# A two-layer decoder trunk: route weights made earlier, alpha·x taken off the matmuls, a fixed order for the layer norm into mixer 1

## The chip, the cores and the metric

The kernel runs on one core of one Trainium2 chip. The metric is the device time of one execution in microseconds (us). Engines are named as in the profile: PE is TensorE's matmuls, PEld its weight loads, DVE is VectorE, ACT is ScalarE, POOL is GpSimd, SP is SyncE, whose queue issues the transfers.

## The reference

256 tokens of 1024 features pass through two layers, all in fp32. Each layer is a mixer and a mixture of experts, and each of these is followed by a layer norm over its input, scaled by alpha, plus its output:

```python
for layer in range(2):
    mix = ab_mixer(x, ...) if layer % 2 == 0 else nsa_mixer(x, ...)
    x = layer_norm(DN_ALPHA * x + mix, ln1_g[layer], ln1_b[layer])
    ffn = hier_moe(x, ...)          # 32 experts in 4 groups, each token routed to 2 of one group
    x = layer_norm(DN_ALPHA * x + ffn, ln2_g[layer], ln2_b[layer])
```

`ab_mixer` is a gated MLP beside a latent attention, `nsa_mixer` an attention with three branches (compressed blocks, selected blocks, window) whose compressed keys and values come from two small networks with weights of their own. `hier_moe` softmaxes the group logits, takes the best group and its top two experts, and gives each expert's output a weight ("route weight" below).

## The kernel before

**Weights and the ring.** All weights come from HBM in slots of 1 MB (128 partitions x 2048 fp32). SBUF holds a ring of 23 places of that size. `Ring` issues the slots on SP's queue at L124, one after the other in the order of a list: for a mixer the string `ORDER[l]`, for the experts slots 0 to 11 of each of eight quads of four experts (`QUADS`). A slot's issue waits until the place it goes to has been freed, and everything behind it on the queue waits too. An entry `P` of `ORDER` is no transfer but a place taken as working space (for the high and low halves of split weights); names such as `CK0`, `QA`, `X` or `xTh` in it are slots or working places too.

**Products.** An fp32 product is made of three products of halves (`mm3`): each operand is split into a rounded high part and the rest. `Splits` makes the halves of a weight, the high part on ACT (L311), the low part on DVE or POOL (L312). All matmuls have the line of the helper `mm`, L182, so that the tile names tell them apart.

**A layer.** Mixer 0 and mixer 1 run under a scheduler (a plan with costs decides the order of their pieces). At their end `project` multiplies the mixer's output by the output weights `WO0..3` into four PSUM accumulators `acc[t][h]` (t: tokens 0 to 127 or 128 to 255; h: columns 0 to 511 or 512 to 1023); its first step opens each accumulator with alpha·x, matmuls of x with `aident`, alpha times the identity. `close_mixer` finishes it: `raw(t)` copies the accumulators to x and takes the statistics of the layer norm, then come the router's logits, `route`, which selects the experts and returns a function that makes the route weights later (L1254 to L1264, 8 small DVE steps and 3 on ACT for each half of the tokens), `rank`, and the first `pick`. `places` makes a one-hot matrix of the tokens of a quad; `pick` multiplies it with x to gather these tokens (`w`, 32 rows an expert); the affine part of the norm (L493) and the second half of the first pick are done in between.

**The experts.** For each quad in turn: `gate_up` (k = 0..7, one slot each, slots 0 to 7, `psC<-ring,w`; after each k a function `between(k)` puts other work in), `activate`, `pick` for the next quad (`psT<-p,x`), `turn_hidden`, `back` (which weights the one-hot matrix by the route weights at L1393, turns it with two matmuls at L1397, and makes the weights of the slots' tokens with `psO<-oneh,p`), and then the down product (slots 8 to 11, `psT<-ring,p`), whose results go back to the tokens in `acc2` (psA, psS). Quad 0 differs: after its gate_up, `rest()` makes the route weights of both halves and `back` for quad 0, and after `turn_hidden` four matmuls with `aident` per token half and column half (`psA<-x,aident`, `psS<-x,aident`; an fp32 matmul of 512 columns is two instructions in the trace) add alpha·x to `acc2`, which had been opened with zeros in `close_mixer` (`zerob`).

**Between the layers.** `open_mixer1` makes the layer norm (`ln2`: L562 and L571, two DVE steps for a half of a token half, with one of four such quarters on ACT and POOL at L568 to L570), transposes each quarter (`transpose_x`: PE L329, ACT L332, DVE L333), and makes the first product of mixer 1, `project(t, low, xk)`, with the narrow weights `NAT`, whose halves are made on ACT (L843, four of 128x608) and POOL (L878). `warm(n)` gives PE n matmuls whose result nobody reads; `W3` says how many stand here, behind the first and the second quarter. In the same stretch the scheduler already splits weights `KVC` and `KSW` for mixer 1 (L311, L312).

Of the kernel before, what the change touches and what calls it, by code (L numbers as in the profile page):

```python
# [24 lines left out]
KC = D // 128  # L25
# [17 lines left out]
W3 = (7, 6)  # L43
# [99 lines left out]
def trunk(ctx, tc, a, out):  # L143
# [109 lines left out]
    aident = consts.tile([128, 128], F32, name="aident")  # L253
    idb = consts.tile([128, 128], BF16, name="idb")
    zerob = consts.tile([128, 128], BF16, name="zerob")
# [11 lines left out]
    def more_constants():  # L267
        V.memset(mhalf, -0.5)
        V.memset(mone, -1.0)
        V.memset(oneh, 1.0)  # L270
        V.memset(oneb, 1.0)
        V.memset(zerob, 0.0)
        V.tensor_scalar(aident, ident, ALPHA, None, op0=ALU.mult)
        V.tensor_copy(maskb, tri[:, 128:256])
        V.tensor_copy(trib, tri[:, 0:128])
# [172 lines left out]
    def project(l):  # L448
# [27 lines left out]
    def close_mixer(l, rb, acc, step, products):  # L476
# [50 lines left out]
        for h in range(2):  # L527
            mm(acc2[0][h], zerob, idb[:, None, :].to_broadcast([128, 4, 128]), True, False)
        warm(2)
# [5 lines left out]
        for h in range(2):  # L535
            mm(acc2[1][h], zerob, idb[:, None, :].to_broadcast([128, 4, 128]), True, False)
        warm(W1[0])
# [297 lines left out]
    def open_mixer1(acc, g, b, mr):  # L835

        wn = []
        for i in range(4):
# [4 lines left out]
            S.activation(hi, src, AF.Copy)  # L843
# [16 lines left out]
        late = []  # L860

        def after(t, h):
            low = transpose_x(xh, xl, t, h)
            if late:
                late.pop()()
            late.append(low)
            if (t, h) == (0, 0):
                warm(W3[0])
            if (t, h) == (0, 1):
                warm(W3[1])  # L870
                project(0, 0, xh)
            if (t, h) == (1, 0):
                project(0, 0, xl)

        ln2(acc, g, b, mr, after)
        late.pop()()
# [3 lines left out]
        project(1, 0, xh)  # L880
        project(1, 0, xl)
# [508 lines left out]
    def back(q, rt, dd, tr, often=True):  # L1390

        d, dw = dd[:, 0:256], (p2() if dd.shape[1] == 256 else dd[:, 256:512])[:, 0:256]
        V.tensor_tensor(dw.rearrange("p (t e s) -> p t e s", t=2, e=4), d.rearrange("p (t e s) -> p t e s", t=2, e=4),  # L1393
                        rt[1][:, :, 4 * q:4 * q + 4, None].to_broadcast([128, 2, 4, 32]), op=ALU.mult)
        p = ps(tr)
# [13 lines left out]
    def gather(q, rt, base, tr):  # L1409
# [5 lines left out]
        return xg, *back(q, rt, dd, tr, often)  # L1415
# [62 lines left out]
    def moe_layer(l, rt, acc, begun):  # L1478
# [3 lines left out]
        gs, late = [(begun[0], None, None)], begun[1:]  # L1482
# [7 lines left out]
        def quad(i):  # L1490
# [4 lines left out]

            def between(k):
                nonlocal rb
                if i == 0 and k >= KC // 2:
                    late[0].pop(0)()
                    if k == KC - 1:  # L1500
                        late[0].pop(0)()
                if k in (2, 4):
                    flush(2)
                if k == 4:
                    dds.append(places(nq, rt, 0.0))
                if k == 5 and i == 3 and l == 0:
# [3 lines left out]
            if i == 0:  # L1510
                gs = [late[1]()]
            hs = activate(hp, [g[2] for g in gs])
            ngs, hts = [], None
            for c in range(nn):
                xg = halves_of(w4())
                pick(dds[c], xg)()
                if c + 1 < nn:
                    dds.append(places(nq, rt, -32.0 * (c + 1)))
                if c == 0:
                    hts = turn_hidden(hs)  # L1520
                    if i == 0:
                        for t in range(2):
                            for h in range(2):
# [169 lines left out]
```

## Time and profile before

| | |
|---|---|
| median of 3 runs | 700.41 us (700.06 to 701.95) |
| the profiled execution | 700.38 us, its span 698.7 us |
| mean granted TensorE clock | 0.956 |
| busy, of the span | PE 619.1 us, DVE 284.3, ACT 204.5, POOL 49.6 |
| moved by DMA | 235.62 MB, mean 337 GB/s |

The profile is that of one execution; its own time is 1.7 us over its span. The times of all rows below are counted from the start of the span. At the 420 GB/s of the stretches in which DMA is full, the 235.62 MB would take 561 us; PE is busy for 619 us. Neither fills the span: there are stretches in which the one waits for the other.

### The profile page before, as it was taken

How to read it: one execution, taken by the hardware profiler on the slowest of the kernel's cores; microseconds unless marked ns; L12 is line 12 of the kernel's file. 1: busy time of each engine (PE TensorE's matmuls, PEld its weight loads, DVE VectorE, ACT ScalarE, POOL GpSimd, SP SyncE). 2: the span in 40 equal slices, each digit the busy share in tenths (PEclk: the TensorE clock that was granted, in tenths of full speed). 3: DMA queues.
4: the chain of work that ended last, by engine and by line, in shares of the span. 5: the costliest groups of instructions: out<-in, count | busy, mean ns of one | idle time of the engine just before them, and what ended most of it. 6: DMA issues, size and time to landing. Idle time of an engine off the chain costs nothing. (4 is left out here: it accounts for less than half of the span.)

```text
span 698.7 us, 11137 instructions
## 1 busy us (share of the span) xinstructions
PE 619.1 (89%) x4459; PEld 386.7 (55%) x4459; DVE 284.3 (41%) x709; ACT 204.5 (29%) x514; POOL 49.6 (7%) x56
## 2 busy tenths in 40 slices
PE   7799999799999685887999999999799899897883
PEld 5678676464555141423988776685554554644331
DVE  4757736522222120206848897444422212312116
ACT  5554534121111010103546676431111111202011
POOL 4611000000000000002420000000000000000002
PEclk9999999989999988997999999999899999999797
DMA  8946879949999999999498450399689999999961
GB/s 344 418 184 247 334 264 380 398 189 425 419 420 418 423 420 416 421 420 416 161 422 342 127 235 1 129 394 401 280 353 420 420 422 421 420 419 422 414 266 60
DMA packets 34068, 235.62 MB, mean 337 GB/s; under 512 B 3920, under 2 KB 4688, under 8 KB 6224
## 3 DMA queue, kind: packets, MB, share of 16 engines
q1 hardware_dynamic: 34000, 234.75, 82.7%
q8 instruction: 38, 0.62, 0.4%
q14 instruction: 30, 0.25, 0.1%
HBM read 233.69 MB, written 1.05 MB: 336 GB/s over the span
## 5 line engine op out<-in xcount | busy, mean ns | idle before, releaser
L182 PE MATMUL psC<-ring,w 128*32 128x512 f32 (+1 forms) x1040 | 132.5, 618 | 24.5 <-PEq L1299 13.1
L182 PEld LDWEIGHTS psC<-ring,w 128*32 128x32 f32 (+1 forms) x1040 | 31.2, 114 | 90.0 <-issue 48.5
L182 PE MATMUL psA<-ring,ring 128*128 128x256 f32 (+1 forms) x480 | 80.1, 315 | 0.0
L182 PE MATMUL psT<-ring,p 128*32 128x512 f32 (+1 forms) x608 | 68.8, 587 | 3.1 <-DMA ring<-in_moe 2.2
L182 PEld LDWEIGHTS psA<-ring,ring 128*128 128x128 f32 x480 | 67.5, 193 | 6.5 <-issue 1.8
L182 PEld LDWEIGHTS psT<-p,x 128*128 128x128 f32 x512 | 64.5, 208 | 10.9 <-issue 10.1
L182 PE MATMUL psT<-p,x 128*128 128x128 f32 x512 | 67.3, 295 | 0.0
L1437 DVE SCALAR_TENSOR_TENSOR p<-p,psC 128x256 f32<-128x256 f32 x16 | 6.7, 421 | 133.5 <-ACT p L1436 133.3
L317 DVE TENSOR_TENSOR p<-psT,p 128x256 fp32r<-128x256 f32 x72 | 30.5, 424 | 62.8 <-ACT p L316 62.8
L1436 ACT ACTIVATE p<-psC 128x256 f32<-128x256 f32 x16 | 6.1, 383 | 170.2 <-PE psC L182 170.2
L316 ACT ACTIVATE p<-psT 128x256 fp32r<-128x256 f32 x72 | 27.5, 383 | 63.2 <-PE psT L182 42.2
L290 POOL TENSOR_TENSOR sm<-sm,mhalf 128x1 f32<-128x1 f32 (+1 forms) x12 | 7.7, 647 | 511.4 <-DVE sm L287 280.6
L182 PEld LDWEIGHTS psA<-p,k 128*128 128x128 f32 x144 | 25.2, 192 | 30.1 <-issue 17.6
L182 PE MATMUL psA<-p,k 128*128 128x256 f32 x144 | 39.4, 313 | 1.6 <-DVE sm L1560 1.6
L312 DVE TENSOR_TENSOR ring<-ring,ring 128x1024 fp32r<-128x1024 f32 (+1 forms) x28 | 36.0, 1301 | 8.0 <-ACT ring L311 7.7
L182 PEld LDWEIGHTS psT<-ring,p 128*32 128x32 f32 x608 | 17.3, 111 | 37.6 <-issue 25.3
L182 PE MATMUL psS<-ring,ring 128*128 128x416 f32 (+3 forms) x128 | 32.0, 384 | 2.0 <-ACT ring L311 1.5
L182 PE MATMUL psO<-ring,ring 128*64 128x256 f32 (+3 forms) x248 | 32.2, 349 | 1.1 <-DVE ring L333 0.7
L311 ACT ACTIVATE ring<-ring 128x1024 fp32r<-128x1024 f32 (+1 forms) x32 | 31.8, 1031 | 3.6 <-issue 1.3
L182 PE MATMUL psS<-p,k 128*128 128x256 f32 x144 | 29.9, 288 | 0.0
L1377 DVE COPY w<-psT 128x512 f32<-128x512 f32 x16 | 11.1, 691 | 44.2 <-PE psT L182 44.2
L1111 ACT ACTIVATE ring<-psS,sm 128x128 f32<-128x128 f32 (+1 forms) x64 | 26.2, 420 | 7.8 <-DVE sm L1102 7.7
(282 smaller groups left out, 844.4 us busy)
## 6 DMA issues: line engine op xcount, KB each, us to landing
ring<-in_moe SPq DMA_DIRECT2D x192, 1024.0 KB, 19.5
ring<-in_m SPq DMA_DIRECT2D x23, 1024.0 KB, 10.0
ring<-in_vec SPq DMA_DIRECT2D x2, 1024.0 KB, 18.1
ring<-in_m SPq DMA_DIRECT2D x2, 832.0 KB, 6.0
x<-in_x SPq DMA_DIRECT2D x2, 512.0 KB, 5.2
out<-x SPq DMA_DIRECT2D x4, 256.0 KB, 2.0
ring<-in_m SPq DMA_DIRECT2D x1, 768.0 KB, 15.0
ring<-in_m SPq DMA_DIRECT2D x1, 736.0 KB, 18.9
```

The costliest lines, as they stand in the source:

```text
L182: T.matmul(o, lhsT, rhs, start=start, stop=stop, skip_group_check=True)
L290: G.tensor_tensor(r, t, mhalf[:, :n], op=ALU.pow)
L311: S.activation(hi, src, AF.Copy)
L312: (sub or V).tensor_tensor(lo, src, hi.bitcast(F32), op=ALU.subtract)
L316: S.activation(hi, src, AF.Copy)
L317: V.tensor_tensor(lo, src, hi.bitcast(F32), op=ALU.subtract)
L1111: S.activation(p[:, i * w:(i + 1) * w], sx[c, u][:, i * w:(i + 1) * w], AF.Exp, bias=nb[:, i0 + i:i0 + i + 1], accum_out=su[:, i0 + i:i0 + ...
L1377: (S.activation(dst, p[0], AF.Copy) if f == 0 else V.tensor_copy(dst, p[0]))
L1436: S.activation(e, p[:, 0:256], AF.Tanh, scale=0.5)
L1437: V.scalar_tensor_tensor(e, e, 1.0, p[:, 0:256], op0=ALU.add, op1=ALU.mult)
```

## The change

It has four parts.

1. **alpha·x without matmuls.** The `aident` matmuls go. In `project` the first product opens the accumulator, and `raw(t)` computes x = alpha·x + acc on DVE, with the statistics then taken from x in SBUF. For the experts, ACT writes alpha·x into `acc2` (`residual`), for columns 0 to 511 during quad 0's gate_up at k = 7, for the others after `back`. The matmuls with `zerob` that opened `acc2` become as many more `warm` matmuls.
2. **Route weights early.** `rest` is split: `shares`, called at k = 1 of quad 0's gate_up, makes the route weights and the weighted one-hot matrix of quad 0; `back` comes after gate_up as before, without the weighting. For the later quads the weighted matrix is made at k = 4 (`onehots`).
3. **Into mixer 1.** `ln2` isn't called: all four quarters of the norm are two DVE steps each (`halves`), in an order written out with the transposes, products and ACT's high halves; the low halves of `NAT` move from POOL to DVE; `W3` falls from 7 and 6 to 4 and 3. A `no_sync_barrier` (an order for the scheduler, no wait on the chip) keeps mixer 1's own pieces behind it.
4. **The list of layer 1.** `CK0` and `CK1` come before `QA Y Q1`, `CV1` and `CV0` a little earlier too. Smaller: `router_prep` of layer 1 moves from quad 3 to quad 5 of layer 0, and the scratch for dynamic DMA is 1024 in place of 512.

```diff
-W3 = (7, 6)
+W3 = (4, 3)
...
-         "NAT1 P P NAT0 P KSW xTl xTh P P KVC P Q0 P P X Z P QA Y Q1 P P P CK0 CK1 CV1 CV0 Q2 P P QB Q3 M P M  "
+         "NAT1 P P NAT0 P KSW xTl xTh P P KVC P Q0 P P X Z CK0 CK1 QA Y Q1 CV1 P P CV0 P P Q2 P P QB Q3 M P M  "
...
         def products(t, i):
             k = ks[i]
-            if i == 0:
-                for h in range(2):
-                    mm(acc[t][h], aident, x[:, t, HALF[h]], True, False)
...
-                mm3(acc[t][h], y, w, False, i == KC - 1)
+                mm3(acc[t][h], y, w, i == 0, i == KC - 1)
...
         def raw(t):
 
             for h in range(2):
-                S.activation(x[:, t, HALF[h]], acc[t][h], AF.Copy)
-            return x[:, t], *stats(acc[t])
+                V.scalar_tensor_tensor(x[:, t, HALF[h]], x[:, t, HALF[h]], ALPHA, acc[t][h], op0=ALU.mult, op1=ALU.add)
+            return x[:, t], *stats([x[:, t, HALF[h]] for h in range(2)])
...
-        def rest():
+        def shares():
             weights0()
             weights1()
-            return (xg, *back(0, rt, dd, "O"))
-
-        return rt, acc2, (xg, [second] + affines, rest)
+            return weighted(0, rt, dd, p2()[:, 0:256])
+
+        return rt, acc2, (xg, [second] + affines, shares, lambda dw: (xg, *back(dd, dw, "O")))
...
+        def halves(t, h):
+
+            xs, (mean, r) = x[:, t, HALF[h]], mr[t]
+            V.scalar_tensor_tensor(xs, acc[t][h], mean, g[:, HALF[h]], op0=ALU.subtract, op1=ALU.mult)
+            V.scalar_tensor_tensor(xs, xs, r, b[:, HALF[h]], op0=ALU.mult, op1=ALU.add)
+            late[t, h] = transpose_x(xh, xl, t, h)
...
+        high(0)
+        halves(0, 0)
+        warm(W3[0])
+        high(1)
+        halves(0, 1)
+        warm(W3[1])
+        high(2)
+        high(3)
+        project(0, 0, xh)
+        halves(1, 0)
+        late[0, 0]()
+        halves(1, 1)
+        late[0, 1]()
+        project(1, 0, xh)
+        project(0, 0, xl)
+        late[1, 0]()
+        late[1, 1]()
+        project(1, 0, xl)
         for hi, lo, src, _ in wn:
-            G.tensor_tensor(lo, src, hi.bitcast(F32), op=ALU.subtract)
+            V.tensor_tensor(lo, src, hi.bitcast(F32), op=ALU.subtract)
...
+            def residual(h):
+                for t in range(2):
+                    S.activation(acc[t][h], x[:, t, HALF[h]], AF.Copy, scale=ALPHA)
+
+            def onehots(c):
+                dd = places(nq, rt, -32.0 * c)
+                dds.append((dd[:, 0:256], weighted(nq, rt, dd[:, 0:256], dd[:, 256:512])))
+
             def between(k):
                 nonlocal rb
+                if i == 0 and k == 1:
+                    late[1] = late[1]()
                 if i == 0 and k >= KC // 2:
                     late[0].pop(0)()
                     if k == KC - 1:
                         late[0].pop(0)()
+                        residual(0)
...
             if i == 0:
-                gs = [late[1]()]
+                gs = [late[2](late[1])]
...
                     hts = turn_hidden(hs)
-                    if i == 0:
-                        for t in range(2):
-                            for h in range(2):
-                                mm(acc[t][h], aident, x[:, t, HALF[h]], False, False)
-                ngs.append((xg, *back(nq, rt, dds[c], "O")))
+                ngs.append((xg, *back(*dds[c], "O")))
+            if i == 0:
+                residual(1)
...
             m = open_mixer1(acc, *gb, mr)
+        tc.no_sync_barrier()
         mixer1(*m)
```

The first place where the order changes is PE's row at the end of gate_up of quad 0, layer 0 (psC is gate_up's accumulator, psO what `back` makes, psT first the pick and then the down product). Before:

```order
L182 MATMUL psC_1136<-ring_699,w_152_1121 32x512 x4
L1397 MATMUL psO_1251<-ident,k_149_1112 128x128 x2
L182 MATMUL psO_1251<-oneh,p_163_1249 128x1 x2
L182 MATMUL psT_1265<-p_158_1175,x 128x128 x8
L182 MATMUL psT_1275<-p_158_1175,x 128x128 x8
L1449 MATMUL psC_1285<-ident,p_167_1260 128x128 x2
L182 MATMUL psA_1033<-x,aident 128x512
L182 MATMUL psA_1034<-x,aident 128x512
L182 MATMUL psS_1035<-x,aident 128x512
L182 MATMUL psS_1036<-x,aident 128x512
L1397 MATMUL psO_1294<-ident,p_158_1175 128x128 x2
L182 MATMUL psO_1294<-oneh,p_158_1175 128x1 x2
```

and after the change:

```order
L182 MATMUL psC_1128<-ring_695,w_152_1113 32x512 x4
L1400 MATMUL psO_1246<-ident,k_149_1104 128x128 x2
L182 MATMUL psO_1246<-oneh,p_156_1155 128x1 x2
L182 MATMUL psT_1260<-p_159_1189,x 128x128 x8
L182 MATMUL psT_1270<-p_159_1189,x 128x128 x8
L1452 MATMUL psC_1280<-ident,p_167_1255 128x128 x2
L1400 MATMUL psO_1284<-ident,p_159_1189 128x128 x2
L182 MATMUL psO_1284<-oneh,p_159_1189 128x1 x2
L182 MATMUL psT_1295<-ring_697,p_167_1255 32x512 x4
```

The four matmuls with `aident` are gone between `turn_hidden` (psC from ident) and the next quad's `back`; the matmul with `oneh` now reads a matrix (`p_156`) that was made during gate_up. The same holds for layer 1.

The second place is DVE's row over the same gate_up (`rt` and `w_121` are the route weights, `w_152` the first pick, the lines on x the affine part of the norm). Before, from the second half of the pick on:

```order
L1383 TENSOR_SCALAR w_152_1121<-psT_1162,col 128x128 x2
L1358 TENSOR_TENSOR p_158_1175<-rk_1103,cst 128x256
L493 TENSOR_TENSOR x<-x,psT_1183 128x512 x2
L493 TENSOR_TENSOR x<-x,psT_1196 128x512 x2
L493 TENSOR_TENSOR x<-x,psT_1209 128x512 x2
L493 TENSOR_TENSOR x<-x,psT_1216 128x512 x2
L1254 TENSOR_SCALAR rt_1056<-rt_1056 128x1
L1256 TENSOR_TENSOR rt_1056<-rt_1056 128x1
L1259 SCALAR_TENSOR_TENSOR rt_1056<-rt_1056 128x1
L1260 RECIPROCAL rt_1056<-rt_1056 128x1
L1261 TENSOR_SCALAR rt_1056<-rt_1056 128x1
L1262 SCALAR_TENSOR_TENSOR rt_1056<-rt_1056 128x1
```

and after the change:

```order
L1262 SCALAR_TENSOR_TENSOR rt_1085<-rt_1085 128x1
L1263 TENSOR_SCALAR rt_1085<-rt_1085 128x32
L1264 SCALAR_TENSOR_TENSOR w_121_1009<-rt_1085 128x32
L1392 TENSOR_TENSOR p_156_1155<-k_149_1104,w_121_1009 128x256
L1383 TENSOR_SCALAR w_152_1113<-psT_1176,col 128x128 x2
L1358 TENSOR_TENSOR p_159_1189<-rk_1095,cst 128x256
L1392 TENSOR_TENSOR p_159_1189<-p_159_1189,w_121_1009 128x256
L486 TENSOR_TENSOR x<-x,psT_1198 128x512 x2
L486 TENSOR_TENSOR x<-x,psT_1211 128x512 x2
L486 TENSOR_TENSOR x<-x,psT_1224 128x512 x2
L486 TENSOR_TENSOR x<-x,psT_1231 128x512 x2
```

Before, the sixteen small steps from L1254 to L1264 (eight for each token half; the first six of them end the first fence) stand behind the last affine row, and the weighting of the one-hot matrix (L1393) behind them. After, the last of these steps, the weighting (now L1392) and that of the next quad stand ahead of the four affine rows.

The third place is DVE's row at the opening of mixer 1 (ring places hold the gain, the bias, the transposed x and split weights). Before:

```order
L571 SCALAR_TENSOR_TENSOR x<-x,sm_4369,ring_4081 128x512
L333 TENSOR_TENSOR ring_4162<-psT_4395,ring_4167 128x4x128
L562 SCALAR_TENSOR_TENSOR x<-psS_1035,sm_4372,ring_4081 128x512
L312 TENSOR_TENSOR ring_4184<-ring_4203,ring_4184 128x1024
L571 SCALAR_TENSOR_TENSOR x<-x,sm_4375,ring_4081 128x512
L333 TENSOR_TENSOR ring_4162<-psT_4411,ring_4167 128x4x128
L312 TENSOR_TENSOR ring_4214<-ring_4203,ring_4214 128x1024
L333 TENSOR_TENSOR ring_4162<-psT_4435,ring_4167 128x4x128
L312 TENSOR_TENSOR ring_4243<-ring_4116,ring_4243 128x1024
L333 TENSOR_TENSOR ring_4162<-psT_4451,ring_4167 128x4x128
L312 TENSOR_TENSOR ring_4261<-ring_4116,ring_4261 128x1024
```

and after the change:

```order
L329 TENSOR_TENSOR ring_4154<-psT_4381,ring_4159 128x4x128
L853 SCALAR_TENSOR_TENSOR x<-psS_1028,sm_4366,ring_4073 128x512
L854 SCALAR_TENSOR_TENSOR x<-x,sm_4369,ring_4073 128x512
L329 TENSOR_TENSOR ring_4154<-psT_4395,ring_4159 128x4x128
L329 TENSOR_TENSOR ring_4154<-psT_4417,ring_4159 128x4x128
L329 TENSOR_TENSOR ring_4154<-psT_4426,ring_4159 128x4x128
L880 TENSOR_TENSOR ring_4085<-ring_4098,ring_4085 128x608
L880 TENSOR_TENSOR ring_4093<-ring_4098,ring_4093 128x608
L880 TENSOR_TENSOR ring_4104<-ring_4079,ring_4104 128x608
L880 TENSOR_TENSOR ring_4171<-ring_4079,ring_4171 128x608
```

DVE has two steps more of the norm (the quarter that ACT and POOL had) and the four low halves of `NAT` (128x608); the low halves of `KVC` and `KSW` (128x1024), which stood between the transposes' rows, follow behind them.

## Rows read from the trace of the kernel before

**Rows 1.** Windows: busy us of each engine, granted clock, DMA share, GB/s.

```profile
20.00:40.00 20.00, 15.62 (x64) 11.33 (x63) 12.98 (x25) 8.21 (x21) 8.31 (x12) 0.91 0.89 360
140.00:146.00 6.00, 6.00 (x29) 6.00 (x29) 1.06 (x3) 1.25 (x3) 0.00 (x0) 0.50 0.68 279
142.00:152.00 10.00, 10.00 (x53) 7.29 (x55) 1.18 (x3) 1.36 (x3) 0.00 (x0) 0.79 0.21 84
152.00:154.00 2.00, 2.00 (x24) 0.64 (x20) 0.42 (x1) 0.67 (x2) 0.00 (x0) 1.00 0.51 106
154.00:332.00 178.00, 147.38 (x1120) 69.95 (x1110) 39.96 (x93) 28.05 (x65) 6.74 (x9) 0.93 1.01 420
342.00:447.00 105.00, 104.46 (x774) 79.24 (x774) 77.05 (x215) 62.01 (x203) 4.88 (x2) 1.00 0.53 211
448.00:500.00 52.00, 46.36 (x293) 34.36 (x292) 23.61 (x80) 12.24 (x26) 1.10 (x2) 0.94 0.99 399
500.00:510.00 10.00, 10.00 (x66) 5.82 (x69) 1.61 (x4) 2.13 (x5) 0.00 (x0) 0.94 0.16 50
510.00:642.00 132.00, 126.58 (x1082) 67.34 (x1075) 30.27 (x73) 23.39 (x56) 0.00 (x0) 1.00 1.01 421
```

**Rows 2.** Timeline, PE, quad 0 of layer 0: start, length.

```profile
134.51 0.44 PE L1397 MATMUL psO<-ident,k 128*128 128x128 f32 x2
139.16 0.92 PE L182 MATMUL psO<-oneh,p 128*128 128x1 f32 x4 [4.22 <-DVE p L1393]
139.95 6.76 PE L182 MATMUL psT<-p,x 128*128 128x128 f32 x32
...
146.76 1.88 PE L182 MATMUL psA<-x,aident 128*128 128x512 f32 x4
...
150.19 0.38 PE L1397 MATMUL psO<-ident,p 128*128 128x128 f32 x2
...
150.85 1.06 PE L182 MATMUL psT<-ring,p 128*32 128x512 f32 x8
```

**Rows 3.** Timeline, DVE, quad 0 of layer 0.

```profile
138.68 0.42 DVE L1393 TENSOR_TENSOR p<-k,w 128x256 f32<-128x256 f32 x1
```

**Rows 4.** Timeline, SP queue: the issues around both gaps.

```profile
121.94 13.02 SPq L124 DMA_DIRECT2D ring<-in_moe  x8
...
151.97 1.19 SPq L124 DMA_DIRECT2D ring<-in_moe  x2
...
507.85 0.33 SPq L124 DMA_DIRECT2D ring<-in_moe  x1
```

**Rows 5.** Timeline, PE, layer 1: quad 0, then the next pick.

```profile
495.76 1.02 PE L182 MATMUL psO<-oneh,p 128*128 128x1 f32 x4 [4.23 <-DVE p L1393]
496.64 5.94 PE L182 MATMUL psT<-p,x 128*128 128x128 f32 x32
...
519.72 3.84 PE L182 MATMUL psT<-p,x 128*128 128x128 f32 x32
```

**Rows 6.** Timeline, ACT, raw(1) of layer 0.

```profile
110.86 1.30 ACT L484 ACTIVATE x<-psS 128x512 f32<-128x512 f32 x2 [1.51 <-PE psS L182]
```

**Rows 7.** What SP waited for: total us, times, longest.

```profile
SPq L124 <- DVE ring L1140: 36.0, 1, 36.0
```

**Rows 8.** Timeline, DVE, POOL and PE, opening of mixer 1.

```profile
326.20 0.75 DVE L571 SCALAR_TENSOR_TENSOR x<-x,sm,ring 128x512 f32<-128x512 f32 x1
...
336.83 1.93 DVE L312 TENSOR_TENSOR ring<-ring,ring 128x1024 fp32r<-128x1024 f32 x1
...
343.47 1.21 DVE L312 TENSOR_TENSOR ring<-ring,ring 128x1024 fp32r<-128x1024 f32 x1
...
330.83 9.27 POOL L878 TENSOR_TENSOR ring<-ring,ring 128x608 fp32r<-128x608 f32 x4
...
331.43 1.46 PE L182 MATMUL psT<-idb 128*128 128x512 bf16 x6
...
342.53 2.68 PE L182 MATMUL psA<-ring,ring 128*128 128x256 f32 x21
```

More of the change, by code (lines that the diff above doesn't have):

```diff
@@ L271, in more_constants @@
         V.memset(oneb, 1.0)
-        V.memset(zerob, 0.0)
-        V.tensor_scalar(aident, ident, ALPHA, None, op0=ALU.mult)
         V.tensor_copy(maskb, tri[:, 128:256])
@@ L526, in close_mixer @@
         acc2 = [[ps("A"), ps("A")], [ps("S"), ps("S")]]
-        for h in range(2):
-            mm(acc2[0][h], zerob, idb[:, None, :].to_broadcast([128, 4, 128]), True, False)
-        warm(2)
+        warm(4)
         xt = transposed(nn[1][0], True)
@@ L534, in close_mixer @@
         o1 = logits(l, xt)
-        for h in range(2):
-            mm(acc2[1][h], zerob, idb[:, None, :].to_broadcast([128, 4, 128]), True, False)
-        warm(W1[0])
+        warm(W1[0] + 2)
         weights1 = route(scaled(1, o1), 1, selb, w32)
@@ L842, in open_mixer1 @@
             hi, lo = ring.get(key)[:, 0:608], ring.get(key)[:, 1024:1632]
-            S.activation(hi, src, AF.Copy)
             wn.append((hi, lo, src, key))
@@ L858, in project, with high @@
                 mm(pn[t][:, 256:304], ident[:, V_GATE:V_GATE + 1].to_broadcast([128, 128]), vec[:, 0:48], False, False)
[L860 to L876, printed above, removed]
+        late = {}
+        def halves(t, h):
[3 more added lines that the diff above has]
+            late[t, h] = transpose_x(xh, xl, t, h)
+        def high(i):
+            hi, _, src, _ = wn[i]
+            S.activation(hi, src, AF.Copy)
+        high(0)
[16 more added lines that the diff above has]
+        project(1, 0, xl)
         for hi, lo, src, _ in wn:
-            G.tensor_tensor(lo, src, hi.bitcast(F32), op=ALU.subtract)
+            V.tensor_tensor(lo, src, hi.bitcast(F32), op=ALU.subtract)
         ring.free(("R", 0))
-        project(1, 0, xh)
-        project(1, 0, xl)
         for t in range(2):
@@ L1388, in pick, with weighted, back @@
         return lambda: half(1)
-    def back(q, rt, dd, tr, often=True):
-        d, dw = dd[:, 0:256], (p2() if dd.shape[1] == 256 else dd[:, 256:512])[:, 0:256]
+    def weighted(q, rt, d, dw):
         V.tensor_tensor(dw.rearrange("p (t e s) -> p t e s", t=2, e=4), d.rearrange("p (t e s) -> p t e s", t=2, e=4),
                         rt[1][:, :, 4 * q:4 * q + 4, None].to_broadcast([128, 2, 4, 32]), op=ALU.mult)
+        return dw
+    def back(d, dw, tr, often=True):
         p = ps(tr)
@@ L1414, in gather @@
         pick(dd, xg)()
-        return xg, *back(q, rt, dd, tr, often)
+        return xg, *back(dd[:, 0:256], weighted(q, rt, dd[:, 0:256], dd[:, 256:512]), tr, often)
     def gate_up(l, q, xgs, between):
@@ L1481, in moe_layer @@
         order = QUADS[l]
-        gs, late = [(begun[0], None, None)], begun[1:]
+        gs, late = [(begun[0], None, None)], list(begun[1:])
         pending = []
@@ L1504, in between @@
                 if k == 4:
-                    dds.append(places(nq, rt, 0.0))
-                if k == 5 and i == 3 and l == 0:
+                    onehots(0)
+                if k == 5 and i == 5 and l == 0:
                     rb = router_prep(1, "T")
@@ L1515, in quad @@
                 xg = halves_of(w4())
-                pick(dds[c], xg)()
+                pick(dds[c][0], xg)()
                 if c + 1 < nn:
-                    dds.append(places(nq, rt, -32.0 * (c + 1)))
+                    onehots(c + 1)
                 if c == 0:
                     hts = turn_hidden(hs)
-                    if i == 0:
-                        for t in range(2):
-                            for h in range(2):
-                                mm(acc[t][h], aident, x[:, t, HALF[h]], False, False)
-                ngs.append((xg, *back(nq, rt, dds[c], "O")))
+                ngs.append((xg, *back(*dds[c], "O")))
+            if i == 0:
+                residual(1)
             for c0, slots in ((0, (8, 9)), (512, (10, 11))):
```

4 lines of the change are left out of this document (1 added, 3 removed).

## The prediction

> **What bounds the kernel now.** I read the windows first, for DMA's share. From 154 to 332 us and from 510 to 642 us DMA is full at 420 GB/s, and from 448 to 500 us nearly so [rows 1]. There a transfer can start only when one has ended, and PE is partly idle (147 of 178 us), so time saved on an engine is worth nothing there unless DMA's stretch as a whole starts earlier. Outside them engines set the pace, and three places count.
>
> First, quad 0 of layer 0: between 142 and 154 us DMA is idle for 10 x 0.79 + 2 x 0.49 = 8.9 us, while PE is busy throughout [rows 1]. The timelines say why. PE ends gate_up, turns the one-hot matrix at 134.51, then stands 4.22 us for DVE's L1393, which comes after the route weights; the pick then takes 6.76 us and the matmuls with aident run from 146.76 to 150.19; the down product starts at 150.85 [rows 2, 3]. SP had issued eight slots while gate_up freed its places, up to about 135, and then nothing until 151.97, when the down product frees the next place [rows 4]. DMA's backlog runs out at 142 + 2.1 = 144.1 and it restarts at 154 - 1.0 = 153.0, some 1.0 us after the issue.
>
> Second, quad 0 of layer 1, alike: 10 x 0.84 = 8.4 us without transfers, PE's wait 4.23, the pick 5.94, the next issue at 507.85 [rows 1, 4, 5]. With 1.0 us from issue to restart, DMA was dry from about 500.5.
>
> Third, mixer 1: PE is busy for 104.46 of 105 us up to 447, and SP stands 36.0 us in one wait, for a step of the last attention outputs (L1140); these free the places of the first expert slots [rows 1, 7]. I call the end of that wait, 447, the release. What PE saves before it moves the rest.
>
> **The change, part by part.** The profiled execution took 700.38 us, 0.03 under the median, so sums against it hold for the median too.
>
> *Quad 0, both layers.* Removed are the wait (4.22 and 4.23 us) and the aident matmuls (150.19 - 146.76 = 3.43 us each). The pick follows the wait: its 6.76 and 5.94 us stand against 3.84 for the same 32 matmuls later [rows 2, 5], and the granted clock of 140 to 146 us is 0.50, that is 1.2 GHz [rows 1]. Without the wait I take 3.84, a gain of 2.92 and 2.10. So slot 8's issue moves by 10.6 us in layer 0 and by 9.8 in layer 1: to 141.4 and 498.1, the restarts to 142.4 and 499.1, ahead of the dry points 144.1 and 500.5 by 1.7 and 1.4 us. The gap closes, and more than the gap isn't gained: **-8.9** and **-8.4**.
>
> What the moved work costs: the route weights are some 4.2 us of DVE and ACT steps, now begun at k = 1 of a gate_up that lasts over 13 us (eight issues, one for each k, in 13.02 us [rows 4]). DVE's affine rows are queued behind them, and the pick waits for those; they end as late as their transposes on PE let them, so I cost this at nothing, and at 4.2 us if DVE doesn't catch up. ACT's residual copies cover what aident did: two between k = 7 and the down product, two behind `back`, each like the copies at L484, 0.65 us [rows 6]; the products into acc2 come after the first down results, so nothing waits. In the later quads the weighting at k = 4 removes a wait that DMA hides: nothing.
>
> The Trainium skill, "TensorE: Matmul & The Clock Gate", section "HAM oscillation", says that a PE that waits for data falls to half rate and begins the next stretch cold. Rows 1 and 2 agree (0.50 behind the wait of 4.22 us). By that page the pick runs at full rate once the wait is gone, as in the sum; without it the picks stay as long as they are, which is the first rival below.
>
> *The project of layer 0.* ACT's copy at 110.86 waited for PE [rows 6], so PE sets its end, and the eight instructions with aident there are the same as those of quad 0: -3.43. raw(1) gets dearer: statistics followed the first ACT copy (0.65), now they follow two DVE steps from PSUM and SBUF, at 0.75 by L571 [rows 8]: +0.85. Everything behind it up to 142 us, the slots freed by gate_up and DMA's dry point with it, comes **-2.6** earlier. At least -1.0, if DMA's backlog there doesn't let the issues take effect; at most -3.4.
>
> *The opening of mixer 1.* The last products waited for POOL: its low halves of NAT run from 330.83 for 9.27 us, to 340.1 [rows 8], and PE's opening ends at 342.5, where mixer 1's products begin [rows 8]; four of these, at 2.68 / 21 = 0.13, were done within it, so it stands for 342.0. On DVE a low half costs 608/1024 of L312's 1.21 us alone, 0.72, or 1.15 by its 1.93 beside POOL [rows 8]; POOL is now out, so 4 x 0.72 = 2.9 us. DVE also gets the fourth quarter, 2 x 0.75. Laid out by hand with these durations from the statistics on, and with transposes, copies and products as long as they are now: DVE ends the norm at 331.5, the last transposed low part at 335.3, the low halves at 338.1; PE then has two of six groups of products to come and ends at 341.3, against 342.0. **-0.7**. Bounds: +1.7 with low halves at 1.15; -2 if the first transposes run at full clock. The six warm matmuls that go are about 1.5 us [rows 8] in time in which PE waited for DVE: nothing by themselves.
>
> The Trainium skill, "SBUF — State Buffer", section "Who interferes with whom", says that DVE with two SBUF operands and GpSimd lock each other out of a shared port. The trace agrees: L312 takes 1.21 us with POOL out and 1.93 with POOL in [rows 8]. By this rule the four halves cost 2.9 us, as in the sum; without it, as DVE ran beside POOL, 4.6.
>
> *Mixer 1.* Eight aident instructions go before the release, 3.43 us. In their place the built order has eight more 512-column products of project ahead of it; a warm matmul of that width is 1.46 / 6 = 0.24 [rows 8], so +1.9. PE is full, so the net is **-1.5**. Bounds: 0 and -3.4. The slots CK and CV move on SP's queue past QA, Y and Q1, which are working places; their first use on PE is late enough in either order: nothing. After the release DMA is full until the gap; project's saving and raw(1) there only change the margin.
>
> *The rest.* A later router_prep and the scratch size lie in DMA-bound time: nothing. From 510 on DMA paces; PE's down product starts 9.8 us earlier against DMA's 8.4, so PE doesn't become the bound.
>
> Sum: -8.9 - 2.6 - 0.7 - 1.5 - 8.4 = -22.1, so 700.4 - 22.1 = **678.3 us**.
>
> **The rivals.**
>
> *The gap closes only in part.* The margins are 1.7 and 1.4 us. If the picks stay at 1.2 GHz, the gaps left are 2.9 - 1.7 = 1.2 and 2.1 - 1.4 = 0.7: 680.2 us. If the weights aren't done in time either (DVE's queue late, so the wait stays): 4.2 more each, 688.6. For it: the half clock began with the wait, but I can't see that the wait alone caused it. Against: over 13 us of gate_up cover 4.2 us of DVE work.
>
> *The project's saving isn't passed on.* If issues before 142 us don't follow PE, the 2.6 shrinks to 1.0, and if mixer 1's release hangs on DVE or ACT rather than PE, 1.5 goes too: 681.4. Against: PE is busy 104.46 of 105.
>
> *The opening gets dearer.* DVE as the only engine of the norm, low halves at 1.15 and a cold PE: +1.7 in place of -0.7, 680.7 us.
>
> *Slower: mixer 1 loses its packing.* The barrier forbids that its splits are interleaved with the opening, and slots and working places come in another order, so the scheduler makes another plan. In mixer 0 PE reaches 15.62 of 20 us, 78%, from 20 to 40 [rows 1]. At that share 104.46 us of work take 134, +29: 707.7 us. It decides when the share falls below 104.46 / (104.46 + 22.1) = 83% over the whole mixer. Against: the working places are in use late only at the start, and DVE (77 of 105 us) and ACT (62) have room [rows 1]; a wait there would be some us, not 22.
>
> *More is gained*: all terms at their better bounds, 674.0.
>
> **Chances.** The forecast with its own range 674 to 684 holds 0.74 and includes the half-clock picks, the project's and the opening's rivals at their prices (some 0.08 each); gaps that remain for the most part, 684 to 690, 0.10; mixer 1 some us worse, 684 to 695, 0.06; much worse, slower than before, 0.04; better than 674, 0.06. The range for 8 in 10 is 671 to 688. A difference under 0.3% (2 us) can't be told from none; faster 0.93, same 0.03, slower 0.04.
>
> **What the profile after would show.** Quad 0: no wait for DVE in front of psO from oneh, a pick of about 3.8 us, DMA's share about 1.0 through both former gaps, the second batch of issues within 2 us of the first. Opening: no POOL row for low halves, DVE's at 0.72, PE's opening ending 0.7 us sooner after the statistics. Mixer 1: opening to release about 103 us at a PE share near 99%. The prediction is wrong if DMA still pauses in quad 0 (then look at the pick's duration and at the releaser of psO), or if mixer 1 shows idle PE (then at what its first weights' halves wait for).

## The result, and the profile after

The changed kernel takes 670.8 us (median of 4 runs, 670.0 to 671.3) against 700.4 of before, a ratio of 0.957 with a 95% interval of 0.9555 to 0.9589. That is 29.6 us faster, where 22.1 were forecast; the range began at 671.0. The profiled execution has a span of 668.9 us.

The windows of the changed kernel, with the columns of [rows 1], over both quads 0, the experts and mixer 1:

```profile
131.00:142.00 11.00, 11.00 (x102) 7.08 (x98) 4.38 (x11) 4.57 (x11) 0.00 (x0) 1.00 1.01 422
142.00:152.00 10.00, 10.00 (x87) 5.66 (x86) 1.75 (x4) 0.98 (x2) 0.00 (x0) 1.00 1.02 420
152.00:322.00 170.00, 138.51 (x1034) 67.13 (x1033) 40.16 (x88) 26.94 (x62) 2.90 (x6) 0.92 1.01 420
326.00:434.00 108.00, 105.37 (x778) 79.69 (x777) 84.05 (x219) 65.97 (x208) 5.65 (x2) 1.00 0.49 180
478.00:490.00 12.00, 12.00 (x109) 7.54 (x102) 5.08 (x13) 4.57 (x11) 0.00 (x0) 1.00 1.01 420
490.00:500.00 10.00, 10.00 (x87) 5.66 (x86) 1.60 (x4) 0.98 (x2) 0.00 (x0) 1.00 1.02 423
510.00:612.00 102.00, 100.89 (x875) 54.45 (x874) 23.79 (x57) 18.93 (x45) 0.00 (x0) 1.00 1.01 421
```

DMA is full through both quads 0, where it had stopped for 8.9 and 8.4 us. Mixer 1 has 2.6 us in which PE isn't busy, where it had 0.5. The timeline of PE in both quads 0, which answers to [rows 2, 5]:

```profile
131.08 0.44 PE L1400 MATMUL psO<-ident,k 128*128 128x128 f32 x2
131.35 0.51 PE L182 MATMUL psO<-oneh,p 128*128 128x1 f32 x4
131.72 3.82 PE L182 MATMUL psT<-p,x 128*128 128x128 f32 x32
...
136.24 3.64 PE L182 MATMUL psT<-ring,p 128*32 128x512 f32 x32
...
478.62 0.44 PE L1400 MATMUL psO<-ident,k 128*128 128x128 f32 x2
...
479.26 3.82 PE L182 MATMUL psT<-p,x 128*128 128x128 f32 x32
...
483.78 3.64 PE L182 MATMUL psT<-ring,p 128*32 128x512 f32 x32
```

PE no longer waits for L1393 in front of psO, the pick takes 3.82 us, no matmul reads aident. From the end of gate_up to the down product it is 136.24 - 131.08 = 5.2 us in layer 0 and as many in layer 1, where it was 16.3 and 15.6.

Milestones read from the timelines (start of the row named, us). The prediction's terms are added up to each:

| | before | after | moved | predicted |
|---|---|---|---|---|
| quad 0 of layer 0: gate_up ends | 134.51 | 131.08 | -3.4 | -2.6 |
| its down product begins | 150.85 | 136.24 | -14.6 | -13.2 |
| last statistics of layer 0 | 324.01 | 309.85 | -14.2 | -11.5 |
| mixer 1's products begin | 342.53 | 326.61 | -15.9 | -12.2 |
| release (next slot issue) | 447.10 | 434.29 | -12.8 | -13.7 |
| quad 0 of layer 1: gate_up ends | 491.10 | 478.62 | -12.5 | -13.7 |
| its down product begins | 506.73 | 483.78 | -22.9 | -23.5 |
| PE's last matmul ends | 687.55 | 657.76 | -29.8 | -22.1 |

Up to the release the forecast is 0.9 us from the milestone, but with errors of both signs on the way, so that this closeness is in part luck. From there to the end, PE gained 17.0 us where 8.4 were forecast: that is where it failed.

### The profile page after: what moved, and what is told of

It is laid out like the page before. It is cut to its first block, busy times and chain, and to the rows that moved or that the text cites. A ratio compares the mean times of both kernels' runs of the same rounds, so it can differ in the third digit from the quotient of the medians.

```text
span 668.9 us, 11035 instructions
## 1 busy us (share of the span) xinstructions
PE 599.8 (90%) x4421; PEld 375.2 (56%) x4421; DVE 293.4 (44%) x720; ACT 204.0 (31%) x513; POOL 38.6 (6%) x50
## 5 line engine op out<-in xcount | busy, mean ns | idle before, releaser
L182 PE MATMUL psC<-ring,w 128*32 128x512 f32 (+1 forms) x1040 | 135.1, 628 | 26.6 <-DMA ring<-in_moe 13.5
L182 PEld LDWEIGHTS psT<-p,x 128*128 128x128 f32 x512 | 59.5, 195 | 11.9 <-issue 10.9
L182 PE MATMUL psT<-p,x 128*128 128x128 f32 x512 | 62.4, 281 | 0.9 <-ACT k L1404 0.9
```

The source lines that it names most:

```text
L182: T.matmul(o, lhsT, rhs, start=start, stop=stop, skip_group_check=True)
```

## The experiments

Each was timed against the kernel before on the same chip. The letters of the theories are those of the recorded expectations: theory A says that PE paces layer 1 from quad 0 to the end, theory B, the prediction's, that DMA does. The ratio of the changed kernel is 0.9555 to 0.9589; where another row's interval overlaps it, the two times alone don't tell the kernels apart.

| | what is different | median, us | ratio to before, 95% |
|---|---|---|---|
| 1 | changed, late weights in layer 1 | 676.7 | 0.9640 to 0.9687 |
| 2 | changed, late weights in layer 0 | 670.9 | 0.9544 to 0.9585 |
| 3 | changed, no split on POOL in mixer 1 | 668.5 | 0.9529 to 0.9582 |
| 4 | changed, old slot list | 675.1 | 0.9613 to 0.9653 |
| 5 | changed, no barrier | 674.6 | 0.9604 to 0.9646 |
| 6 | before, early route weights of quad 0 alone | 686.9 | 0.9782 to 0.9826 |
| 7 | before, early weighting of later quads alone | 693.7 | 0.9873 to 0.9925 |
| 8 | before, projects without aident alone | 698.8 | 0.9960 to 0.9985 |
| 9 | changed, old opening, list, no barrier | 672.1 | 0.9569 to 0.9603 |
| 10 | before, new opening, list, barrier alone | 700.7 | 0.9988 to 1.0014 |
| 11 | as 9, and no split on POOL | 671.7 | 0.9572 to 0.9608 |
| 12 | before, experts without aident alone | 694.7 | 0.9903 to 0.9941 |

**1 and 2. Who paces the experts of each layer.** The later quads' one-hot matrices are weighted again behind the pick, in one layer (the edit of experiment 1; experiment 2 has `l == 0`):

```diff
-                dds.append((dd[:, 0:256], weighted(nq, rt, dd[:, 0:256], dd[:, 256:512])))
+                late_w = partial(weighted, nq, rt, dd[:, 0:256], dd[:, 256:512])
+                dds.append((dd[:, 0:256], late_w if l == 1 else late_w()))
...
+                d, dw = dds[c]
-                ngs.append((xg, *back(*dds[c], "O")))
+                ngs.append((xg, *back(d, dw() if callable(dw) else dw, "O")))
```

> The changed kernel, but in layer 1 the later quads' one-hot matrices are weighted where they were before the change, behind the pick. Theory A: after quad 0 of layer 1 it is PE, not DMA, that paces the rest; the eight waits of 0.46 to 1.01 us that come back (6.1 us in the trace of before) are paid, less 0.9 us of waits for ACT that stand in their place now: 5 to 6 us over the changed kernel's 670.8, so 676 to 677. Theory B, that of the prediction: DMA paces there and hides them, 670.8 within 0.5.

> The same in layer 0 alone, where six waits of 0.68 us come back (4.1 us). Theory A (PE paces layer 1 only; in layer 0 DMA paces from quad 1 on): 670.8 within 0.7. Theory C, PE paces the experts of both layers: 674 to 675.

Layer 1 cost 5.9 us over the 670.8. Layer 0 cost nothing by the median, 670.9; its five runs lie between 666.1 and 671.6, and theory C's 674 to 675 is outside its interval. The waits of PE in experiment 1 from 483 to 612 us (what it waited for, total us, times, longest):

```profile
PE psO L182 <- DVE p L1392: 5.4, 7, 1.0
```

and in experiment 2 from 138 to 311 us:

```profile
PE psC L182 <- DMA ring<-in_moe: 9.5, 11, 1.5
...
PE psO L182 <- DVE p L1392: 4.1, 6, 0.7
```

Both have the waits for the weighting. In layer 0 PE also waits 9.5 us for slots in gate_up, and in the changed kernel, from 137 to 310 us, 4.0 us more:

```profile
PE psC L182 <- DMA ring<-in_moe: 13.5, 16, 1.4
```

So there a wait for DVE (4.1 us) only comes in place of one for DMA. In layer 1 there is no wait for DMA that could give way. Theory A holds for layer 1, theory B for layer 0, theory C (PE paces both) falls.

**7. The same from the other side.** The kernel before, with the weighting of the later quads at k = 4 (`if i`: from the third quad on, since in this kernel the route weights aren't made yet at k = 4 of the first):

```diff
                 if k == 4:
                     dds.append(places(nq, rt, 0.0))
+                    dws.append(weighted(nq, rt, dds[-1][:, 0:256], dds[-1][:, 256:512]) if i else None)
```

> The kernel before with the one-hot matrices of the later quads weighted at k = 4 (from quad 1 on, both layers), nothing else. Theory A (PE paces layer 1 to the end, DMA paces layer 0): the eight waits of layer 1, 6.1 us, are gained, nothing of the six in layer 0: 694 to 695. Theory B, that of the prediction: hidden by DMA in both layers, 700.5.

6.8 us faster, a little more than theory A's 6.1, which lies within the interval (5.3 to 8.9); theory B's 0 is far outside. From 511 to 642 us PE is left with

```profile
PE psT L182 <- ACT k L1407: 0.9, 2, 0.4
```

instead of seven waits of 5.4 us for L1393 (the eighth, of 0.68 us at 663.78, is gone too), and from the down product of quad 0 to PE's end it takes 173.6 us in place of 180.8.

**6 and 12. Quad 0.** Two of its parts alone, on the kernel before. The early route weights:

```diff
-        def rest():
+        def shares():
             weights0()
             weights1()
-            return (xg, *back(0, rt, dd, "O"))
+            return weighted(0, rt, dd, p2()[:, 0:256])
...
+                if i == 0 and k == 1:
+                    late[1] = late[1]()
```

> The kernel before with one thing of the change: quad 0's route weights are made at k = 1 of its gate_up, in both layers. The matmuls with aident stay. If the wait alone made the pick slow, PE reaches the down product 7.1 us earlier in layer 0 (4.2 + 2.9) and 6.3 in layer 1; DMA's gap of layer 0 shrinks by 7.1, and layer 1 ends 6.3 earlier: 700.5 - 13.4 = 687. If the picks stay at 1.2 GHz for another reason: 8.4 in all, 692.

and alpha x by ACT:

```diff
+            def residual(h):
+                for t in range(2):
+                    S.activation(acc[t][h], x[:, t, HALF[h]], AF.Copy, scale=ALPHA)
...
-                    if i == 0:
-                        for t in range(2):
-                            for h in range(2):
-                                mm(acc[t][h], aident, x[:, t, HALF[h]], False, False)
```

> The kernel before with alpha x of the experts written by ACT in place of aident; the projects and the route weights stay. Four matmuls, 3.43 us of PE, go from quad 0 of each layer. Layer 0: DMA's gap shrinks by 3.4. Layer 1, theory A (PE paces): the end comes 3.4 earlier. Together 693.6.

The first gained 13.6 us of 13.4 worked out, the second 6.1 of 6.9. PE's timeline in quad 0 of layer 0, early weights alone:

```profile
133.78 0.44 PE L1403 MATMUL psO<-ident,k 128*128 128x128 f32 x2
...
134.42 3.82 PE L182 MATMUL psT<-p,x 128*128 128x128 f32 x32
...
138.29 1.88 PE L182 MATMUL psA<-x,aident 128*128 128x512 f32 x4
```

and aident alone gone, so that the down product follows the pick:

```profile
139.23 1.01 PE L182 MATMUL psO<-oneh,p 128*128 128x1 f32 x4 [4.22 <-DVE p L1393]
140.10 5.47 PE L182 MATMUL psT<-p,x 128*128 128x128 f32 x32
...
147.22 1.07 PE L182 MATMUL psT<-ring,p 128*32 128x512 f32 x8
```

Without the wait the pick takes 3.82 us, with aident still there; with the wait but without aident it is 5.47. So the wait, and not the matmuls behind it, makes the pick slow, and the DVE work hides under gate_up as worked out.

**8. The projects.** In both layers `raw` adds alpha x on DVE, on the kernel before:

```diff
-                S.activation(x[:, t, HALF[h]], acc[t][h], AF.Copy)
-            return x[:, t], *stats(acc[t])
+                V.scalar_tensor_tensor(x[:, t, HALF[h]], x[:, t, HALF[h]], ALPHA, acc[t][h], op0=ALU.mult, op1=ALU.add)
+            return x[:, t], *stats([x[:, t, HALF[h]] for h in range(2)])
```

> The kernel before with alpha x of the two projects added by raw on DVE in place of the aident matmuls; the experts keep theirs. Layer 0: the prediction says 2.6 us earlier; the trace of the changed kernel shows slot issues 4.0 us earlier at the end of the project and DMA's stream 4 us earlier beyond the gap. Mixer 1: the prediction says 1.5 earlier at the release. So 696.4 by the prediction, 695 if the 4.0 hold; 698 or more if mixer 1 is planned worse.

Only 1.7 us, less than the prediction's terms (4.1) or the sum with the 4.0 (5.5). The number is near the third, 698 or more, but not for its reason: mixer 1 isn't longer. The rows that follow are of its profiled execution, the fastest of the ten (696.1 us). Its slots up to the project's end came 2.7 us earlier (24.5 us from the issue at 67.5 to that at 91.9, before 27.2), but some of it is given back at the first gate_up. PE's timeline:

```profile
116.15 2.46 PE L182 MATMUL psT<-k,x 128*128 128x128 f32 x16 [0.87 <-DVE sm L1280]
118.53 4.83 PE L182 MATMUL psC<-ring,w 128*32 128x512 f32 x32
123.30 2.05 PE L182 MATMUL psT<-k,x 128*128 128x128 f32 x16
```

The 32 matmuls of k = 0 to 3 take 4.83 us, at half clock for a part (granted 0.50 from 118 to 120 us; 3.64 in the changed kernel, where the same wait stands ahead of them), and the wait for DVE ahead of this has grown from 0.29 to 0.85 us, which is raw's price. From the opening to the release mixer 1 took 0.6 us less, where 1.5 were forecast.

**3, 4 and 5. Mixer 1 in the changed kernel.** PE waits 2.07 us for a step of the compress branch. DVE, POOL and PE there in the changed kernel:

```profile
336.69 4.56 DVE L308 TENSOR_TENSOR ring<-ring,ring 128x1024 fp32r<-128x1024 f32 x2
341.29 0.68 DVE L951 TENSOR_TENSOR w<-psA,w 64x512 fp32r<-64x512 f32 x1
...
336.90 3.27 POOL L308 TENSOR_TENSOR ring<-ring,ring 128x1024 fp32r<-128x1024 f32 x1 [25.01 <-ACT ring L307]
344.96 2.38 POOL L308 TENSOR_TENSOR ring<-ring,ring 128x1024 fp32r<-128x1024 f32 x1 [4.78 <-ACT ring L307]
...
346.37 3.11 PE L182 MATMUL psA<-ring,ring 128*128 128x256 f32 x24 [2.07 <-DVE w L951]
```

The second of DVE's two low halves runs beside POOL's: together they take 4.56 us, where two alone take 2.36 (experiment 3). The first L951 comes behind them, and PE behind L951. Experiment 3 gives POOL's two halves to DVE:

```diff
-POOL = ((1, 3), (9, 10))
+POOL = ((1, 3), ())
```

> The changed kernel with no weight split of mixer 1 on POOL: the two low halves that POOL makes go to DVE. Theory D: PE's 2.1 us of idle time in mixer 1 come from DVE's low half, which takes 3.42 us beside POOL's in place of 1.2, with the first step of the compress branch queued behind it; without POOL the idle time goes and the release comes 2 us earlier: 668 to 669. Theory E: the wait is set by the late landing of the weights that are split there; POOL doesn't matter, 670.8, or up to 1 more for DVE's added work.

668.5 us. PE's only waits from 326 to 433 us that are over 0.3 us:

```profile
PE psA L182 <- DVE ring L961: 0.4, 1, 0.4
```

and from the last statistics to the release it takes 122.3 us in place of 124.4. In the trace the wait goes with POOL's halves, as theory D has it; the interval of the time overlaps that of the changed kernel, so the 2.3 us are a difference of medians. Whether the wait comes at all hangs on 1 us of timing. Experiment 2 has the same mixer 1, with POOL's halves:

```profile
336.47 2.36 DVE L308 TENSOR_TENSOR ring<-ring,ring 128x1024 fp32r<-128x1024 f32 x2
...
337.67 3.43 POOL L308 TENSOR_TENSOR ring<-ring,ring 128x1024 fp32r<-128x1024 f32 x1 [25.25 <-ACT ring L307]
...
344.42 3.11 PE L182 MATMUL psA<-ring,ring 128*128 128x256 f32 x24 [0.33 <-DVE w L951]
```

Here POOL begins 1.20 us after DVE's pair, not 0.21: DVE loses nothing, PE waits 0.33 us, and mixer 1 takes 106.0 us in place of 107.7. Experiment 4 puts the list back:

```diff
-X Z CK0 CK1 QA Y Q1 CV1 P P CV0 P P Q2
+X Z P QA Y Q1 P P P CK0 CK1 CV1 CV0 Q2
```

> The changed kernel with the slot list of layer 1 as before (CK and CV behind QA, Y, Q1 and the working places). Theory E: Q1, which comes two slots later in the new list, lands some 5 us late for its split; with the old list PE's idle time of 2.1 us in mixer 1 goes, 668 to 669. Theory D: only the meeting of POOL's and DVE's splits counts; the list moves them both and the time stays at 670.8 within 1. The prediction priced the list at nothing.

Neither theory: 4.3 us slower, and the intervals don't overlap. ACT and PE in it:

```profile
341.40 2.00 ACT L307 ACTIVATE ring<-ring 128x1024 fp32r<-128x1024 f32 x2 [11.91 <-DMA ring<-in_m]
...
349.00 5.15 PE L182 MATMUL psA<-ring,ring 128*128 128x256 f32 x24 [5.34 <-DVE w L951]
```

ACT takes its work in the program's order. It stands 11.9 us before a split whose slot hasn't landed, the compress steps (L950) are queued behind that split, and PE waits 5.3 us for them. In the new list ACT stands 4.7 us at that place. Without the barrier (experiment 5):

```diff
             m = open_mixer1(acc, *gb, mr)
-        tc.no_sync_barrier()
         mixer1(*m)
```

> The changed kernel without the no_sync_barrier ahead of mixer 1, so that the scheduler again puts halves of KVC and KSW between the steps of the opening. Theory F, the barrier is what lets the opening end earlier, at a smaller price in mixer 1: three low halves of 1.2 us stand ahead of the norm on DVE, the opening ends 2 to 4 us later, PE's idle time of 2.1 us in mixer 1 goes: 671 to 673. Theory G, the barrier is what makes mixer 1 longer (107.8 us from the opening's end to the release, 104.7 before) and costs more than it brings: 668 or less.

3.8 us slower, 674.6, more than theory F's and against G. PE's wait for x in it, from 308 to 440 us:

```profile
PE psT L325 <- DVE x L854: 7.7, 2, 4.1
```

and ACT's row ahead of it:

```profile
317.93 2.00 ACT L307 ACTIVATE ring<-ring 128x1024 fp32r<-128x1024 f32 x2 [4.31 <-DMA ring<-in_m]
```

The halves of KVC and KSW come between the steps of the norm, and PE waits 7.7 us for x where it waits 3.1 in the changed kernel. Theory F counted only the time of these halves on DVE. The larger part is that they wait: ACT stands 4.3 us before a high half whose slot hasn't landed, and the low half on DVE and the norm's next step stand behind it.

**9, 10 and 11. The opening, list and barrier as a whole.** Experiment 9 undoes all three in the changed kernel (`open_mixer1` of before, W3 = (7, 6), the old list, no barrier), experiment 10 does them alone on the kernel before, experiment 11 is 9 with POOL as in experiment 3.

> The changed kernel with the opening of mixer 1, W3, the slot list and the missing barrier of the kernel before: the changes to alpha x and to the route weights alone. Theory H: from the last statistics of layer 0 to the release the changed kernel takes 124.4 us, the kernel before 123.1 and that with its projects alone changed 122.6, so the new opening and list cost 1.8 us as a whole, and this kernel is at 669. The prediction's terms (opening 0.7 gained, the list nothing): 671.5.

> The kernel before with the new opening, W3, barrier and slot list alone, aident kept everywhere. Theory H: 1.3 to 1.9 us slower, 702. By the prediction's term: 0.7 faster, 699.8.

> The same as the kernel with the old opening, and no weight split of mixer 1 on POOL. Theory D (POOL's split costs only where it meets DVE's with the compress steps queued behind): in the old order POOL's two splits came behind those steps and PE never waited there, so no gain, within 0.7 us of the kernel with the old opening. If POOL's splits slow DVE there too, 1 to 2 us faster.

672.1 us: by the medians the three bring 1.3 us in the changed kernel, which the overlapping intervals don't tell from nothing, and nothing in the kernel before (700.7). Theory H, that they cost 1.8, is refuted by 9, whose interval begins at 670.6 us; in 10 its 702 isn't reached either. My sum from single profiles had missed that the old opening isn't always 18.5 us long, from the last statistics to mixer 1's products. In experiment 9 it takes 21.3:

```profile
313.29 2.51 ACT L832 ACTIVATE ring<-ring 128x608 fp32r<-128x608 f32 x4 [4.11 <-DMA ring<-in_m]
315.71 0.76 ACT L557 ACTIVATE x<-psS,sm,sm 128x512 f32<-128x512 f32 x1
...
321.61 1.95 DVE L560 SCALAR_TENSOR_TENSOR x<-x,sm,ring 128x512 f32<-128x512 f32 x1
...
323.71 0.63 PE L325 MATMUL psT<-ident,x 128*128 128x128 f32 x4 [2.31 <-DVE x L560]
```

ACT's four high halves of NAT wait for a slot until 313.29, the quarter that ACT makes stands behind them, POOL's two steps behind that. DVE's next step of the norm (L560) then takes 1.95 us beside POOL's low halves, where it takes 0.75 alone, and PE waits 2.3 us more for x. In the opening of before, the slot was there 0.4 us before the norm's first step; here it comes 0.9 after it. In the seven profiles with the old opening it takes 18.5 or 18.6 us in three (before, 6 and 8) and 20.9 to 21.5 in four (7, 9, 11 and 12); in the six with the new opening and the barrier 16.0 to 16.8. Mixer 1 gives a part of that back: 104.0 to 104.6 us with the old order, 106.0 to 107.7 with the new list and the barrier in the changed kernel. Experiment 11 equals 9 within its runs: with the old order POOL's halves do no harm.

## Why the prediction was wrong

**The step that failed** is "From 510 on DMA paces; PE's down product starts 9.8 us earlier against DMA's 8.4, so PE doesn't become the bound", and with it "In the later quads the weighting at k = 4 removes a wait that DMA hides: nothing." I took a full DMA for a pacing DMA. PE's waits in the kernel before, from 154 to 324 and from 510 to 642 us, would have told:

```profile
PE psC L182 <- DMA ring<-in_moe: 11.3, 13, 1.5
...
PE psO L182 <- DVE p L1393: 5.4, 7, 1.0
```

In layer 0 PE waited 13 times for a slot in gate_up, in layer 1 never: its 132 - 126.6 = 5.4 us without work were the waits for the weighting, to the last tenth. DMA was full there and yet ahead of PE: a slot took some 20 us from its issue to its landing, and the last slot was there at about 675 us, some 12.5 us before PE's last matmul ended. In the changed kernel PE waits between 484 and 612 us for

```profile
PE psT L182 <- ACT k L1404: 0.9, 2, 0.4
```

and nothing else. So the price of the weighting was 5.9 to 6.8 us, not nothing (experiments 1 and 7), and the gap of layer 1 was worth PE's time, 9.8 us as worked out and 10.4 in the table, not DMA's 8.4, for the wait and the aident matmuls are PE time. In the table's terms the 17.0 us behind the release are 10.4 up to the down product and 6.9 after it, less 0.3 in gate_up. The room that PE has over DMA is mostly used up by the change: the last slot is there at about 653.4 us, some 4.3 us before PE's last matmul ends.

**Point by point.** *Quad 0* was right: the wait, the pick's clock and aident came out as worked out (experiments 6 and 12), and the gap of layer 0 is closed. *The project of layer 0*: 2.6 forecast; in the changed kernel's slot issues 27.2 - 24.5 = 2.7 less 0.6 for raw, so 2.1; in experiment 8 gate_up ends 1.1 earlier. The other 1.3 us by which gate_up ends earlier in the table stand already at the 31st slot issue (68.0 and 66.7), ahead of all that the change touches; in the 14 profiles that issue lies between 65.3 and 68.7. *The tail of layer 0*, of which the prediction has no term, is 1.3 us shorter from the first row below to the last statistics (10.1 and 8.8 us); its last products in the kernel before ran at half clock, 0.50 from 314 to 320 us. PE's rows there, before:

```profile
313.87 1.94 PE L182 MATMUL psT<-ring,p 128*32 128x512 f32 x8 [0.29 <-DMA ring<-in_moe]
316.36 1.94 PE L182 MATMUL psT<-ring,p 128*32 128x256 f32 x16 [0.56 <-DMA ring<-in_moe]
```

and after:

```profile
301.03 1.06 PE L182 MATMUL psT<-ring,p 128*32 128x512 f32 x8 [0.32 <-DMA ring<-in_moe]
303.51 1.07 PE L182 MATMUL psT<-ring,p 128*32 128x256 f32 x16 [1.42 <-DMA ring<-in_moe]
...
306.08 1.07 PE L182 MATMUL psT<-ring,p 128*32 128x256 f32 x16 [0.35 <-DMA ring<-in_moe]
```

*The opening*: from the last statistics to mixer 1's products 18.5 us before and 16.8 after, 1.8 in place of 0.7 (1.2 if one takes the four products of mixer 1 out of the opening before, as the prediction did). The rows after:

```profile
311.79 0.71 ACT L859 ACTIVATE ring<-ring 128x608 fp32r<-128x608 f32 x1 [4.13 <-DMA ring<-in_m]
...
321.65 2.89 DVE L880 TENSOR_TENSOR ring<-ring,ring 128x608 fp32r<-128x608 f32 x4
...
326.61 8.56 PE L182 MATMUL psA<-ring,ring 128*128 128x256 f32 x70
```

The low halves take 2.89 us on DVE, as forecast, and PE doesn't wait for them. That the last products of before waited for POOL was a wrong reading: PE's one wait among them is for DVE's transposed low part, whose neighbours on DVE were slow beside POOL (1.93 us for 1.21 [rows 8]):

```profile
339.41 0.82 PE L182 MATMUL psO<-ring,ring 128*128 128x304 f32 x4 [0.71 <-DVE ring L333]
```

That the old opening can be longer than 18.5 us (experiment 9) wasn't seen. *Mixer 1*: -1.5 forecast, and it is +3.1: from the opening's end to the release 107.7 us after 104.6 (+2.6 if the four products count to it). Eight aident instructions went and eight products of project came as counted, but this alone is worth -0.6, not -1.5 (experiment 8): the products were priced by a warm matmul in bf16, 0.24 us, and in the trace eight more of them take 2.6 us, some 0.32 each. The new wait behind DVE and POOL costs 2.07 us, and some 1.1 us more aren't broken down. This is the fourth rival (lost packing) in small, and idle PE in mixer 1 is what the prediction had named as a sign of being wrong. The list's price of nothing was wrong in the new order, where it saves 4.3 us (experiment 4). The two terms together, -2.2 forecast, are +1.3 in the profiles. Experiment 9, which undoes the opening, the list and the barrier but not the project, has -1.3 against the -0.7 forecast for these, a difference within the noise. *More is gained* was added up 0.3 too low: with all terms at their better bounds the sum gives 674.3, not 674.0.

**What is left over.** The single parts gain 13.6 + 6.1 + 6.8 + 1.7 + 0.1 = 28.3 us; 1.7 of this can't count twice, since in layer 0 the wait, the pick and aident together (10.6) exceed the gap (8.9). So 26.6 are explained by parts and 29.6 measured. Experiment 9 gives the opening 1.3 in place of 0.1; where the last 1.8 come from isn't settled. Each of the five gains has an interval of 0.9 to 1.8 us either way, so a remainder of this size can't be told from none. Single profiles can't assign it either: in the nine with the projects changed, gate_up of layer 1 ends 42.7 us after the release in five and 44.3 or 44.4 in four, which have a stretch at half clock there.

## What to carry to other kernels

A transfer queue that is full doesn't say that it paces: look whether the engine ever waits for it, and which of the two ends first. Before pricing a removed wait at nothing, find the wait that takes its place; where there is none the wait is paid in full, however small it is each time. And an engine that takes work in order turns one late slot or one slow step into a stall of all that is queued behind (experiments 4 and 5), so an order is to be judged by what stands behind its longest wait.

The version with the lowest median is the changed kernel without POOL's splits in mixer 1: 668.5 us, though its interval overlaps that of the changed kernel.

## What the runs showed of the hardware

That a low half on DVE (two SBUF operands) can be nearly three times as long beside one on POOL: two of them took 4.56 us in place of 2.36, while POOL's own took 3.27 us there and 2.38 a little later. In experiment 2 POOL's began 1.20 us after DVE's pair in place of 0.21, and then DVE's took 2.36 us, as alone, and POOL's 3.43. The rows of before had shown 1.93 for 1.21 [rows 8]. The Trainium skill, "SBUF — State Buffer", section "Who interferes with whom", says that such a pair lock each other out of the shared port; these rows agree, and show that the price of one meeting for DVE varies from nothing to 2.2 us with when POOL begins.

That the half clock (0.50, 1.2 GHz) comes and goes between executions of the same instructions. In layer 1 the changed kernel and experiment 2 are the same program, and PE reaches the first gate_up of both behind the same two waits, of 0.85 and 0.87 us, the second of which ends at 461.38 and at 459.45. The windows behind it, of the changed kernel:

```profile
462.00:466.00 4.00, 4.00 (x25) 2.77 (x27) 1.04 (x6) 1.25 (x5) 0.00 (x0) 0.58 0.93 387
```

and of experiment 2:

```profile
460.00:464.00 4.00, 4.00 (x38) 2.09 (x40) 2.08 (x13) 1.30 (x5) 0.00 (x0) 1.00 0.99 393
```

The clock granted is 0.58 in the one and 1.00 in the other, and the 48 matmuls from there on (16 of the pick and gate_up's first 32) take 7.2 us in the one and 5.6 in the other. What decides it isn't shown.
